# HGRN2 and differential attention on one core: Newton's steps on GpSimd, x's block sums behind the second head's gates, query weights split by VectorE, last heads' transposes with an earlier due time

## The chip, the cores and the metric

The kernel runs on one core of a Trainium2 chip. The time is the device time of one execution in microseconds (us), as the median of several runs. The core's engines work side by side, each through its own queue in order: TensorE (PE, matmuls and transposes), VectorE (DVE), ScalarE (ACT), GpSimd (POOL), and SyncE (SP), which starts most DMAs. They wait for each other by semaphores.

## What is computed

A trunk of two layers over 512 frames of 1024 features (float32, batch 1). The first layer mixes by a gated linear recurrence (HGRN2) of 8 heads, the second by differential attention of 8 heads over keys and values projected after layer one; a squared-ReLU MLP follows each. Every part has an RMS norm before and after. Cut to what matters here:

```python
def rms_norm(x, w):
    y = x * lax.rsqrt(jnp.mean(x * x, axis=-1, keepdims=True) + EPS)
    return y * w

def hgrn2_mixer(h, w_in, lb, gate_norm_w, w_out):
    q, f, i, g = jnp.split(h @ w_in, ...)
    q = silu(q); k = (1 - lb) * sigmoid(-f); log_f = ...
    o = hgrn2_recurrence(q, k, log_f, i)          # S_t = diag(f_t) S_(t-1) + k_t v_t^T, o_t = S_t^T q_t
    return (rms_norm(o, gate_norm_w) * silu(g)) @ w_out

def diff_attn_mixer(h, k, v, w_q, ...):
    o = softmax(q0 k0 + bias) v - lam * softmax(q1 k1 + bias) v
    return rms_norm(o, subln_w) * (1 - lam_init) @ w_out

for layer in range(2):
    h = h + rms_norm(mixer(rms_norm(h, pre)), post)
    h = h + rms_norm(mlp(rms_norm(h, mlp_pre)), mlp_post)
```

The norm of each head's output, in either mixer, and the norm of x at the very start need a reciprocal square root for each frame: a tile of 128 partitions by 4 numbers.

## The kernel before

Activations lie with features on the partitions and 512 frames along the free axis. A float32 product is made of three matmuls: weights and activations are each split into a high part (`whi`, `xhi`, `uhi`, rounded by a ScalarE copy) and a low part (`wlo`, `xlo`, `ulo`, the difference, a VectorE subtraction), and hi x hi, hi x lo and lo x hi are added up in PSUM.

The order of PE's instructions is written out by the class `Plan` (L45): a main generator, and chains that are spawned from it, each of which yields a number or a condition. The numbers are due times in estimated PE time: a chain whose time has come and whose condition holds goes on before the main generator does. The constants `W_...` (L30 to L36) are these due times. PE's order is kept as the plan issues it; the other engines' queues are ordered by a scheduler, with instructions of chains ahead of those of the main generator.

The stages that the change touches:

- **The start.** `first_loads` brings x and the first query weights; `start` (L735) squares x, sums the squares by matmuls (`ps_mc`), takes the reciprocal root `rcol` with `rsqrt_col` (L240), lays it on a diagonal `dg` (L755), and PE spreads it to `rb` with `ps_sp`. All gates of the heads need `rb`. Meanwhile PE works on the projections `qf` of heads 0 and 1 and the values `i`.
- **`rsqrt_col`** makes an estimate by integer arithmetic on the bits (L249) and three Newton steps of three VectorE operations each (L251 to L253). It is called once by `start` and 16 times by `head_norm` (L622), once for each head of either mixer. `head_norm` squares the head's output on ScalarE, calls it, scales the output (`os`, two quarters on VectorE, L632, two on ScalarE, L634), waits `W_HEAD` and transposes with PE (`hn`).
- **`block_sums`** (L695) makes sums and differences of blocks of x for the fast block products of the value and gate projections: eight ScalarE copies into `sums`, then a VectorE subtraction, three times four VectorE operations (`odd`), and four splits (`x0` to `x3`). It is spawned in the main generator (L1058) when `rb` is there.
- **HGRN heads.** `head` (L801) makes the gates, then goes through levels of block size 1 to 64: PE's scores `gl`, on VectorE the products of q and k with the decay (L849, L850) and a masked copy, on GpSimd the product of decays `tt` (L853). Two heads run interleaved. PE meanwhile goes on with projections: `i`, the gate `g` with weights `wg`, the next heads' `qf`.
- **Query weights.** Heads 0 to 3 split by `load_w` (ScalarE copy, VectorE subtraction); heads 4 to 7 by `load_d` (L204): a negated ScalarE copy into the low part, a copy into the high part, and a DMA from GpSimd's queue that adds the weight to the low part.

Of the kernel before, what the change touches and what calls it, by code (L numbers as in the profile page):

```python
# [14 lines left out]
ALU = mybir.AluOpType  # L15
# [16 lines left out]
W_NEW, W_NEWSUM, W_RSTD = 5.8, 9.7, 4.5  # L32
W_GATE_FIRST, W_GATE, W_LEVEL = 10.0, 5.7, 2.15
W_KEYS, W_STATE = 1.5, 0.8
W_HEAD, W_STORE = 11.7, 5.5
W_QK, W_NEXT, W_P, W_PER_TILE, W_PT = 3.6, 0.94, 5.0, 0.66, 2.5  # L36


# [50 lines left out]
def trunk_kernel(ctx: ExitStack, tc: tile.TileContext, x_t, w_qf, w_g, w_gs, w_i, w_is, w_ao, w_kv, w_q, w_bo, w_up, w_us, w_dn,  # L89
# [71 lines left out]
            nc.sync.dma_start(raw[:, i * n:(i + 1) * n, :], src[:, per * pr + i * n:per * pr + (i + 1) * n, :])  # L161
        return raw

    last_split = []

    def split_w(raw, gain, pr, name):

# [27 lines left out]
    def split_b(raw, name):  # L195
# [8 lines left out]
    def load_d(src, ncols, name):  # L204

        out = []
        per = 1024 // ncols
        for pr in range(ncols // 128):
            out += split_d(fetch_w(src, ncols, pr, name), src[:, per * pr:per * (pr + 1), :], f"{name}_{pr}")
        return out  # L210
# [29 lines left out]
    def rsqrt_col(ms, add, out, scale=1.0):  # L240

        n = ms.shape[1]
        x = cp.tile([P, 4], F32, tag="nx", name="nx", bufs=4)[:, :n]
        t = cp.tile([P, 4], F32, tag="nt", name="nt", bufs=4)[:, :n]
        if isinstance(add, float):
            v.tensor_scalar(x, ms, scale, add, op0=ALU.mult, op1=ALU.add)
        else:
            v.scalar_tensor_tensor(x, ms, scale, add, op0=ALU.mult, op1=ALU.add)
        v.tensor_scalar(out.bitcast(I32), x.bitcast(I32), -0.5, 1597463007.0, op0=ALU.mult, op1=ALU.add)  # L249
        for _ in range(3):  # L250
            v.scalar_tensor_tensor(t, out, -0.5, out, op0=ALU.mult, op1=ALU.mult)  # L251
            v.tensor_tensor(t, t, x, op=ALU.mult)
            v.scalar_tensor_tensor(out, t, 1.5, out, op0=ALU.add, op1=ALU.mult)  # L253

    def mean_cols(parts, n, ones):

# [362 lines left out]
                    else:  # L619
                        yield r  # L620

    def head_norm(pool, po, add, name):  # L622

        os = pool.tile([P, 4, P], F32, tag="os", name=f"os_{name}", bufs=2)
        ss = col("ss")
        for c in range(4):
            a.activation(os[:, c, :], po[:, c * P:(c + 1) * P], AF.Square, accum_out=ss[:, c:c + 1])
        y = col("yh")
        rsqrt_col(ss, add, y, 1.0 / P)
        for c in range(4):  # L630
            if c % 2 == 0:
                v.tensor_scalar(os[:, c, :], po[:, c * P:(c + 1) * P], y[:, c:c + 1], None, op0=ALU.mult)  # L632
            else:
                a.activation(os[:, c, :], po[:, c * P:(c + 1) * P], AF.Copy, scale=y[:, c:c + 1])  # L634
        yield W_HEAD
        pt = smt(f"hn_{name}")
        for c in range(4):
            pe.transpose(pt[:, c * P:(c + 1) * P], os[:, c, :], ident)
        yield pt
# [55 lines left out]
    def block_sums(xs, ts):  # L695

        gain = gn[:, G_APRE:G_APRE + 8]
        e, f = sums

        def split(src, sign, n):  # L700
            if n < 3:
                hi, lo = [wp.tile([P, 4, 256], F32R, tag=t, name=f"{t}_x{n}", bufs=8) for t in ("whi", "wlo")]
            else:
                hi, lo = [u[3].rearrange("p j (r t) -> p (j r) t", r=2) for u in (uhi, ulo)]
            a.activation(hi, src, AF.Copy, scale=sign)
            if sign > 0:
                v.tensor_tensor(lo, src, hi.bitcast(F32), op=ALU.subtract)
            else:
                v.scalar_tensor_tensor(lo, src, -1.0, hi.bitcast(F32), op0=ALU.mult, op1=ALU.subtract)
            ts.append([(hi[:, r, :], lo[:, r, :]) for r in range(4)])  # L710

        def odd(n, out, op):

            for r in range(4):
                v.scalar_tensor_tensor(out[:, r], xs[2 * r + 1][:, n * 256:n * 256 + 256], gain[:, 2 * r + 1:2 * r + 2],
                                       out[:, r], op0=ALU.mult, op1=op)

        for r in range(4):
            for n, t in enumerate((e, f)):
                a.activation(t[:, r], xs[2 * r][:, n * 256:n * 256 + 256], AF.Copy, scale=gain[:, 2 * r:2 * r + 1])  # L720
            yield 2.0
        v.tensor_tensor(e, e, f, op=ALU.subtract)
        split(e, 1.0, 0)
        yield 5.0
        odd(1, f, ALU.subtract)
        split(f, 1.0, 1)
        yield 5.0
        odd(1, e, ALU.add)
        split(e, -1.0, 2)
        yield 5.0  # L730
# [61 lines left out]
    def hgrn(hp, w0, xs):  # L792
# [8 lines left out]
        def head(h, pss):  # L801
            if h < 2:
# [8 lines left out]
                                   sg.rearrange("p (c t) -> p c t", c=4), op0=ALU.mult, op1=ALU.mult)  # L811
            v.tensor_tensor(qq.rearrange("p (c t) -> p c t", c=4), qc[:, :, 0:P],
                            tf.rearrange("p (c t) -> p c t", c=4), op=ALU.mult)
            a.activation(qc[:, :, P:192], qq.rearrange("p (c b two) -> p c b two", c=4, two=2)[:, :, :, 1], AF.Copy)
            yield W_GATE if h >= 2 else W_GATE_FIRST
            if h >= 2:
                yield until(("mix", h - 2))
# [70 lines left out]
                    pe.matmul(po[:, c * P:(c + 1) * P], qq[:, c * P:(c + 1) * P], st[:, c - 1, :], start=False, stop=True)  # L888
                yield 0
            done(("po", h))  # L890
            for pt in head_norm(hp, po, EPS, f"a{h}"):
                if isinstance(pt, float):
                    yield pt
            v.tensor_tensor(gg, pt, gg, op=ALU.mult)
# [130 lines left out]
        for p in range(4):  # L1025
            for h in (2 * p, 2 * p + 1):
                if h >= 3 and h % 2:
                    yield until(("rec", h - 3))
                wt = w0 if h == 0 else w1 if h == 1 else load_w(w_qf[h], 256, None, f"qf{h}") if h < 4 else load_d(w_qf[h], 256, f"qf{h}")
                pss = [mmt(f"qf{h}_{n}") for n in range(2)]  # L1030
                if h == 0:
                    w1 = load_w(w_qf[1], 256, None, "qf1")
                    done("w1")
                    for kt in range(8):
                        for n in (1, 0):
                            wmm(pss[n], wt, kt, n * P, xhi, xlo, 0, S, kt == 0, kt == 7)
                        yield 0
                else:
                    for n in (1, 0):
                        for kt in range(8):  # L1040
                            wmm(pss[n], wt, kt, n * P, xhi, xlo, 0, S, kt == 0, kt == 7)
                            yield 0
                spawn(head(h, pss))
            if p == 0:
# [10 lines left out]
                    for i in range(2):  # L1055
                        a.activation(vts[i][:, tt, :], ps[:, i * 256:(i + 1) * 256], AF.Copy, scale=rcol[:, tt:tt + 1])
                yield until("rb")
                spawn(block_sums(xs, ts), 2.0)  # L1058
                wt = load_w(w_g, 256, None, "wg")
                for j in range(2):  # L1060
                    ps = mmt(f"g0_{j}")
# [47 lines left out]
    def attention(ap, f):  # L1109
# [27 lines left out]
        def unit(h, qi, kq, vt, bt, po, mx):  # L1137
# [40 lines left out]
            if qi == 3:  # L1178

                ez = col("ez")  # L1180
                v.scalar_tensor_tensor(ez, mx[:, :, 2], EPS, mx[:, :, 2], op0=ALU.mult, op1=ALU.mult)
                for hn in head_norm(ap, po, ez, f"b{h}"):
                    if isinstance(hn, float):
                        yield hn
                store_u(h, hn)
                yield W_STORE
                done(("amix", h))
# [166 lines left out]
```

## Time and profile before

| | |
|---|---|
| median of 3 runs | 1273.94 us (1272.99 to 1274.47) |
| the profiled execution | 1273.18 us |
| its span in the trace | 1271.4 us |
| PE busy | 1240.0 us (98%) |
| VectorE busy | 825.8 us (65%) |
| ScalarE busy | 673.9 us (53%) |
| GpSimd busy | 95.6 us (8%), 166 instructions |
| mean granted clock of PE | 0.994 |

The span is the time between the first and the last instruction in the trace; the rest of the profiled execution's time lies around it. A granted clock of 1.00 is PE at full speed (2.4 GHz), 0.50 is the lower level (1.2 GHz). A row of the view in order of time gives the start, the duration, the engine, the line and the operation with what it writes and reads; in brackets stands how long the engine had been idle, and what ended that. The numbers of buffers and heads are left out of names there: `os_a` is the scaled output of an HGRN head, `os_b` of an attention head, `qf` the query and forget projections in HGRN, `kq` the key and query ones in attention.

### The profile page before, as it was taken

What the parts mean: (1) busy time and instruction counts of PE and PEld (TensorE: products, weight loads), DVE (VectorE), ACT (ScalarE), POOL (GpSimd) and SP (SyncE); (2) the same over time, 40 slices, a digit from 0 to 9 for tenths busy, and PEclk for the clock granted to TensorE, in tenths of its full rate; (3) what the DMA queues carried; (4) which work ended last, traced back from release to release, by engine and by line L of the source; (5) the groups of instructions that cost most, each with busy time, mean ns of one, the idle gap of its engine ahead of it and who ended that gap; (6) DMA issues with size and microseconds to landing.
All of it is one profiled execution on the core that took longest, in us unless ns stands there. A gap on an engine that the chain in (4) does not pass through costs nothing.

```text
span 1271.4 us, 21443 instructions
## 1 busy us (share of the span) xinstructions
PE 1240.0 (98%) x8440; PEld 1122.8 (88%) x8440; DVE 825.8 (65%) x1654; ACT 673.9 (53%) x1248; POOL 95.6 (8%) x166
## 2 busy tenths in 40 slices
PE   9999999999999999999999999999999999999996
PEld 7788898899988988989999787889998898988996
DVE  7768885866854654636488978664885463663645
ACT  7345546437751733715556877664773371561632
POOL 0102211210000000000100000001000000000000
PEclk9999999999999999999999999999999999999999
DMA  7223557342356663644616322313435355363521
GB/s 253 72 67 92 122 115 184 94 150 68 135 166 124 179 149 95 186 106 115 217 51 203 113 88 79 100 63 105 137 111 158 96 175 122 103 196 74 158 102 67
DMA packets 57303, 158.54 MB, mean 125 GB/s; under 512 B 6354, under 2 KB 8659, under 8 KB 57203
## 3 DMA queue, kind: packets, MB, share of 16 engines
q1 hardware_dynamic: 45920, 120.34, 30.2%
q0 software_dynamic: 11040, 36.71, 13.7%
q8 instruction: 66, 1.08, 0.4%
q14 instruction: 35, 0.28, 0.1%
q10 hardware_dynamic: 242, 0.13, 0.0%
HBM read 147.45 MB, written 9.70 MB: 124 GB/s over the span
## 4 chain that ended last, share of the span: by engine, by line
PE 79%; issue 6%; DMA 6%; DVE 5%; ACT 4%; POOL 0%; SPq 0%; DVEq 0%; ACTq 0%; POOLq 0%
PE dn L114 20%; PE qf L114 7%; PE up L114 7%; PE ux L114 6%; PE kq L114 6%; PE ao_h L114 3%; DMA raw_s<-in_w_us_dram 3%; PE bo_h L114 3%; PE dn_h L114 3%; PE uz L114 3%; PE gl L114 3%; PE v L114 3%; PE g L114 2%; PE lg L114 2%; PE i L114 2%
## 5 line engine op out<-in xcount | busy, mean ns | idle before, releaser
L114 PE MATMUL dn<-uhi,whi_dn 128*128 128x512 f32 x384 | 151.9, 396 | 0.0
L114 PE MATMUL dn<-ulo,whi_dn 128*128 128x512 f32 x384 | 151.9, 396 | 0.0
L114 PE MATMUL dn<-uhi,wlo_dn 128*128 128x512 f32 x384 | 151.9, 395 | 0.0
L200 ACT ACTIVATE whi_a<-raw_a 128x1024 fp32r<-128x1024 f32 x24 | 25.4, 1059 | 118.5 <-PE dn L114 115.6
L114 PEld LDWEIGHTS dn<-uhi,whi_dn 128*128 128x128 f32 x384 | 72.2, 188 | 17.8 <-ACT r L563 0.7
L114 PEld LDWEIGHTS dn<-uhi,wlo_dn 128*128 128x128 f32 x384 | 72.2, 188 | 17.3
L114 PEld LDWEIGHTS dn<-ulo,whi_dn 128*128 128x128 f32 x384 | 72.2, 188 | 16.9
L173 DVE TENSOR_TENSOR wlo_dn<-raw_dn,whi_dn 128x1024 fp32r<-128x1024 f32 x64 | 76.6, 1220 | 5.9 <-ACT whi_dn L172 4.6
L468 DVE TENSOR_TENSOR ulo<-r,uhi 128x1024 fp32r<-128x1024 f32 (+1 forms) x40 | 40.2, 1010 | 53.7 <-ACT uhi L467 53.7
L114 PE MATMUL up<-xhi,wlo_up 128*128 128x256 f32 x256 | 72.1, 281 | 1.0 <-DVE wlo_up L173 1.0
L114 PE MATMUL up<-xhi,whi_up 128*128 128x256 f32 x256 | 72.6, 284 | 0.0
L114 PE MATMUL up<-xlo,whi_up 128*128 128x256 f32 x256 | 71.8, 281 | 0.0
L172 ACT ACTIVATE whi_dn<-raw_dn 128x1024 fp32r<-128x1024 f32 x64 | 65.7, 1051 | 7.1 <-PE up L114 3.0
L114 PE MATMUL dn_h<-uhi,whi_dn 128*128 128x256 f32 x240 | 66.6, 278 | 0.0
L114 PE MATMUL dn_h<-ulo,whi_dn 128*128 128x256 f32 x240 | 66.3, 276 | 0.0
L114 PE MATMUL dn_h<-uhi,wlo_dn 128*128 128x256 f32 x240 | 66.3, 276 | 0.0
L610 DVE TENSOR_TENSOR zacc<-dn,zacc 128x512 f32<-128x512 f32 x32 | 22.1, 691 | 59.1 <-PE dn L114 59.0
L512 POOL DMA_DIRECT2D raw_s<-in_w_us_dram x24 | 20.8, 866 | 490.3 <-DMA raw_s<-in_w_us_dram 288.3
L114 PE MATMUL qf<-xhi,whi_qf 128*128 128x512 f32 x128 | 53.2, 415 | 1.7 <-ACT xhi L679 1.4
L114 PE MATMUL qf<-xhi,wlo_qf 128*128 128x512 f32 x128 | 51.4, 402 | 1.8 <-DMA wlo_qf<-in_w_qf_dram 1.7
L114 PE MATMUL qf<-xlo,whi_qf 128*128 128x512 f32 x128 | 51.4, 401 | 0.3 <-DVE xlo L680 0.3
L200 ACT ACTIVATE whi_t<-raw_a 128x1024 fp32r<-128x1024 f32 x24 | 25.5, 1061 | 49.4 <-PE dn L114 27.2
(531 smaller groups left out, 4133.8 us busy)
## 6 DMA issues: line engine op xcount, KB each, us to landing
raw_dn<-in_w_dn_dram SPq DMA_DIRECT2D x64, 512.0 KB, 4.5
raw_a<-in_w_us_dram SPq DMA_DIRECT2D x24, 512.0 KB, 4.3
raw_s<-in_w_us_dram SPq DMA_DIRECT2D x48, 256.0 KB, 4.4
raw_s<-in_w_us_dram POOLq DMA_DIRECT2D x24, 512.0 KB, 6.4
raw_up<-in_w_up_dram SPq DMA_DIRECT2D x16, 512.0 KB, 4.2
raw_wkv<-in_w_kv_dram SPq DMA_DIRECT2D x16, 512.0 KB, 3.7
raw_qf<-in_w_qf_dram SPq DMA_DIRECT2D x14, 512.0 KB, 4.8
raw_d<-in_w_us_dram SPq DMA_DIRECT2D x12, 512.0 KB, 4.3
```

Of the source, the lines that this page charges most:

```text
L114: nc.tensor.matmul(out, lhsT, rhs, **kw)
L172: last_split[:] = [a.activation(hi, raw, AF.Copy)]
L173: v.tensor_tensor(lo, raw, hi.bitcast(F32), op=ALU.subtract)
L200: a.activation(hi, raw, AF.Copy)
L468: v.tensor_tensor(ulo[pr][:, :, lo:hi], r, uhi[pr][:, :, lo:hi].bitcast(F32), op=ALU.subtract)
L512: g.dma_start(rs, ws[p, :, 0:2, :], accum_op=ALU.add)
L610: v.tensor_tensor(z, pss[n4], z, op=ALU.add)
```

## The change

Four things, in seven pieces of the source:

1. The Newton steps go to GpSimd, as four operations a step: square, product with x, `-0.5 t + 1.5`, product. The estimate stays on VectorE. For 17 calls, 153 VectorE operations leave and 204 on GpSimd come.
2. `block_sums` is spawned by head 1's gate, with the due time `W_GATE_FIRST` = 10, and its eight copies are held on ScalarE until head 1's last gate copy (`odd`, L814) is issued. Its later due times shrink from 5 to 3.
3. Heads 4 to 7 load their query weights with `load_w`: eight negated copies on ScalarE and eight adding DMAs on GpSimd's queue leave, and eight subtractions on VectorE come.
4. The transposes of the last head of each mixer get the due time 9.0 instead of 11.7.

```diff
-W_HEAD, W_STORE = 11.7, 5.5
+W_HEAD, W_HEAD_LAST, W_STORE = 11.7, 9.0, 5.5
...
         for _ in range(3):
-            v.scalar_tensor_tensor(t, out, -0.5, out, op0=ALU.mult, op1=ALU.mult)
-            v.tensor_tensor(t, t, x, op=ALU.mult)
-            v.scalar_tensor_tensor(out, t, 1.5, out, op0=ALU.add, op1=ALU.mult)
+            g.tensor_tensor(t, out, out, op=ALU.mult)
+            g.tensor_tensor(t, t, x, op=ALU.mult)
+            g.tensor_scalar(t, t, -0.5, 1.5, op0=ALU.mult, op1=ALU.add)
+            g.tensor_tensor(out, out, t, op=ALU.mult)
...
-    def head_norm(pool, po, add, name):
+    def head_norm(pool, po, add, name, last):
...
-        yield W_HEAD
+        yield W_HEAD_LAST if last else W_HEAD
...
+        def copies(r):
+            for n, t in enumerate((e, f)):
+                a.activation(t[:, r], xs[2 * r][:, n * 256:n * 256 + 256], AF.Copy, scale=gain[:, 2 * r:2 * r + 1])
...
         for r in range(4):
-            for n, t in enumerate((e, f)):
-                a.activation(t[:, r], xs[2 * r][:, n * 256:n * 256 + 256], AF.Copy, scale=gain[:, 2 * r:2 * r + 1])
+            with tc.issue_after(marks["a"].ins):
+                copies(r)
             yield 2.0
...
-        yield 5.0
+        yield 3.0
...
-            a.activation(qc[:, :, P:192], ..., AF.Copy)
+            odd = a.activation(qc[:, :, P:192], ..., AF.Copy)
+            if h == 1:
+                marks["a"] = odd
+                spawn(block_sums(xs, ts), W_GATE_FIRST)
...
-                wt = w0 if h == 0 else w1 if h == 1 else load_w(w_qf[h], 256, None, f"qf{h}") if h < 4 else load_d(w_qf[h], 256, f"qf{h}")
+                wt = w0 if h == 0 else w1 if h == 1 else load_w(w_qf[h], 256, None, f"qf{h}")
...
-                spawn(block_sums(xs, ts), 2.0)
```

What this does to the queues at three places. PE's own order is the same but for the four transposes `hn` of HGRN's head 7, which stand three matmuls earlier, and SP's is the same.

**VectorE at the start, from the estimate of `rcol` to the diagonal `dg`.** Before:

```order
L246 TENSOR_SCALAR nx<-ps_mc 128x4
L173 TENSOR_TENSOR wlo_wi_347<-raw_wi_344,whi_wi_346 128x1024
L249 TENSOR_SCALAR rcol<-nx 128x4
L173 TENSOR_TENSOR wlo_wg_596<-raw_wg_593,whi_wg_595 128x1024
L251 SCALAR_TENSOR_TENSOR nt<-rcol 128x4
L173 TENSOR_TENSOR wlo_wg_602<-raw_wg_599,whi_wg_601 128x1024
L252 TENSOR_TENSOR nt<-nt,nx 128x4
L707 TENSOR_TENSOR wlo_x_716<-sums_82,whi_x_715 128x1024
L253 SCALAR_TENSOR_TENSOR rcol<-nt,rcol 128x4
L173 TENSOR_TENSOR wlo_qf_0_727<-raw_qf_0_724,whi_qf_0_726 128x1024
L251 SCALAR_TENSOR_TENSOR nt<-rcol 128x4
L715 SCALAR_TENSOR_TENSOR sums_82<-xraw_74,gn,sums_82 128x256
```

After:

```order
L173 TENSOR_TENSOR wlo_wi_338<-raw_wi_335,whi_wi_337 128x1024
L238 TENSOR_SCALAR nx<-ps_mc 128x4
L173 TENSOR_TENSOR wlo_wi_344<-raw_wi_341,whi_wi_343 128x1024
L241 TENSOR_SCALAR rcol<-nx 128x4
L173 TENSOR_TENSOR wlo_wi_350<-raw_wi_347,whi_wi_349 128x1024
L748 TENSOR_SCALAR nrcol<-rcol 128x4
L752 TENSOR_TENSOR dg<-ident,rcol 128x512
L756 COPY rb<-ps_sp 128x512
```

The Newton operations (`nt`, `rcol`) stand on GpSimd, and the splits of the gate's weights (`wlo_wg`), of the sums (`wlo_x`) and of head 2's query (`wlo_qf`) between them are gone from here.

**VectorE behind level 16 of heads 0 and 1** (`q_385` and `k_379` before, `q_388` and `k_382` after, are head 1's; `gl_16` in the masked copy is the level). Before:

```order
L849 TENSOR_TENSOR q_385<-q_385,tt_469 128x16x16
L850 TENSOR_TENSOR k_379<-k_379,tt_469 128x16x16
L825 COPY_PREDICATED sc_462<-mask,gl_16_579 112x16x16
L707 TENSOR_TENSOR wlo_x_838<-sums_83,whi_x_837 128x1024
L849 TENSOR_TENSOR q_371<-q_371,tt_454 128x8x32
L850 TENSOR_TENSOR k_365<-k_365,tt_454 128x8x32
L825 COPY_PREDICATED sc_447<-mask,gl_32_609 96x8x32
L849 TENSOR_TENSOR q_385<-q_385,tt_469 128x8x32
L850 TENSOR_TENSOR k_379<-k_379,tt_469 128x8x32
```

After:

```order
L849 TENSOR_TENSOR q_388<-q_388,tt_472 128x16x16
L704 TENSOR_TENSOR wlo_x_597<-sums_83,whi_x_596 128x1024
L850 TENSOR_TENSOR k_382<-k_382,tt_472 128x16x16
L825 COPY_PREDICATED sc_465<-mask,gl_16_603 112x16x16
L712 SCALAR_TENSOR_TENSOR sums_82<-xraw_74,gn,sums_82 128x256
L712 SCALAR_TENSOR_TENSOR sums_82<-xraw_75,gn,sums_82 128x256
L712 SCALAR_TENSOR_TENSOR sums_82<-xraw_76,gn,sums_82 128x256
L712 SCALAR_TENSOR_TENSOR sums_82<-xraw_77,gn,sums_82 128x256
L173 TENSOR_TENSOR wlo_wg_620<-raw_wg_617,whi_wg_619 128x1024
L173 TENSOR_TENSOR wlo_wg_626<-raw_wg_623,whi_wg_625 128x1024
L849 TENSOR_TENSOR q_374<-q_374,tt_457 128x8x32
L850 TENSOR_TENSOR k_368<-k_368,tt_457 128x8x32
```

Four operations of the block sums and both splits of the gate's weights now stand between the levels of 16 and 32.

**VectorE around the norms of heads 0 and 1** (`os_a_777`, `os_a_809` before; `os_a_802`, `os_a_837` after). Before, from the end of the first chain:

```order
L246 TENSOR_SCALAR nx<-ss 128x4
L253 SCALAR_TENSOR_TENSOR yh<-nt,yh 128x4
L249 TENSOR_SCALAR yh<-nx 128x4
L632 TENSOR_SCALAR os_a_777<-o_769,yh 128x128
L251 SCALAR_TENSOR_TENSOR nt<-yh 128x4
L252 TENSOR_TENSOR nt<-nt,nx 128x4
L253 SCALAR_TENSOR_TENSOR yh<-nt,yh 128x4
L797 TENSOR_TENSOR k_882<-qf_1_737,rb 128x512
L251 SCALAR_TENSOR_TENSOR nt<-yh 128x4
L632 TENSOR_SCALAR os_a_777<-o_769,yh 128x128
L252 TENSOR_TENSOR nt<-nt,nx 128x4
L253 SCALAR_TENSOR_TENSOR yh<-nt,yh 128x4
```

After, the whole of it:

```order
L238 TENSOR_SCALAR nx<-ss 128x4
L241 TENSOR_SCALAR yh<-nx 128x4
L625 TENSOR_SCALAR os_a_802<-o_794,yh 128x128
L238 TENSOR_SCALAR nx<-ss 128x4
L241 TENSOR_SCALAR yh<-nx 128x4
L625 TENSOR_SCALAR os_a_802<-o_794,yh 128x128
L794 TENSOR_TENSOR k_897<-qf_1_762,rb 128x512
L625 TENSOR_SCALAR os_a_837<-o_829,yh 128x128
L803 TENSOR_SCALAR ek_898<-ek_898,oml,lb 128x512
L625 TENSOR_SCALAR os_a_837<-o_829,yh 128x128
L912 TENSOR_TENSOR raw_sgs_1019<-raw_sgs_1019 128x512
L913 TENSOR_TENSOR raw_sgs_1019<-raw_sgs_1019,raw_ags_1018 128x512
```

The second head's `nx` and estimate stand behind the first head's scaling, and head 2's `k` and `ek` behind and between the scalings.

**ScalarE at the same place.** Before:

```order
L634 ACTIVATE os_a_777<-o_769,yh 128x128
L798 ACTIVATE ek_883<-k_882 128x512
L634 ACTIVATE os_a_777<-o_769,yh 128x128
L805 ACTIVATE k_882<-k_882 128x512
L191 ACTIVATE whi_dgs_1018<-raw_sgs_1010 128x512
L634 ACTIVATE os_a_809<-o_801,yh 128x128
L190 ACTIVATE wlo_dgs_1019<-raw_sgs_1010 128x512
L634 ACTIVATE os_a_809<-o_801,yh 128x128
L200 ACTIVATE whi_sgs_1025<-raw_sgs_1010 128x1024
```

After:

```order
L627 ACTIVATE os_a_802<-o_794,yh 128x128 x2
L795 ACTIVATE ek_898<-k_897 128x512
L627 ACTIVATE os_a_837<-o_829,yh 128x128
L802 ACTIVATE k_897<-k_897 128x512
L627 ACTIVATE os_a_837<-o_829,yh 128x128
L191 ACTIVATE whi_dgs_1027<-raw_sgs_1019 128x512
L190 ACTIVATE wlo_dgs_1028<-raw_sgs_1019 128x512
L200 ACTIVATE whi_sgs_1034<-raw_sgs_1019 128x1024
```

The two copies of half weights (`whi_dgs`, `wlo_dgs`) stand behind both scalings of head 1. In attention the same happens once with the copy `at` of head 1's third query tile: it stood ahead of both ScalarE scalings of head 0, and stands behind the first of them.

## Rows read from the trace of the kernel before

**Rows 1.** the page: busy time (share of the span) and instructions of each engine

```profile
PE 1240.0 (98%) x8440; PEld 1122.8 (88%) x8440; DVE 825.8 (65%) x1654; ACT 673.9 (53%) x1248; POOL 95.6 (8%) x166
```

**Rows 2.** PE's waits: what PE waited for, total us, times, longest us

```profile
PE ps_sp L114 <- DVE dg L755: 3.0, 1, 3.0
PE qf L114 <- DMA wlo_qf<-in_w_qf_dram: 1.7, 1, 1.7
PE ao_h L114 <- ACT uhi L643: 1.4, 1, 1.4
PE qf L114 <- ACT xhi L679: 1.4, 1, 1.4
```

**Rows 3.** PE in order of time: start, us, operation [idle before <-releaser]

```profile
11.17 0.51 PE L114 MATMUL qf<-xhi,whi_qf 128*128 128x512 f32 x1 [1.38 <-ACT xhi L679]
...
40.11 2.07 PE L114 MATMUL ps_sp<-dg,ones 128*128 128x512 f32 x2 [3.04 <-DVE dg L755]
```

**Rows 4.** ScalarE in order of time, just before the first of these waits

```profile
9.60 0.91 ACT L720 ACTIVATE sums<-xraw,gn 128x256 f32<-128x256 f32 x2 [0.75 <-DMA xraw<-in_x_t_dram]
```

**Rows 5.** VectorE in order of time, from the first estimate to the diagonal

```profile
31.25 0.16 DVE L249 TENSOR_SCALAR rcol<-nx 128x4 int32<-128x4 int32 x1
31.32 1.22 DVE L173 TENSOR_TENSOR wlo_wg<-raw_wg,whi_wg 128x1024 fp32r<-128x1024 f32 x1
...
39.37 0.68 DVE L755 TENSOR_TENSOR dg<-ident,rcol 128x512 f32<-128x512 f32 x1
```

**Rows 6.** stretches: us, busy PE PEld DVE ACT POOL, granted clock, DMA share, GB/s

```profile
40.00:42.50 2.50, 2.39 (x4) 1.26 (x5) 0.33 (x2) 0.00 (x0) 0.00 (x0) 0.51 0.32 123
42.50:45.00 2.50, 2.50 (x11) 2.02 (x10) 2.47 (x5) 1.33 (x3) 0.00 (x0) 0.81 0.00 0
...
213.00:216.00 3.00, 3.00 (x26) 2.87 (x25) 1.21 (x4) 0.56 (x2) 0.00 (x0) 1.00 1.08 273
```

**Rows 7.** GpSimd in order of time, products of heads 2 and 3

```profile
102.53 0.65 POOL L853 TENSOR_TENSOR tt<-tt 128x4 f32<-128x4 f32 x1
...
115.37 0.20 POOL L853 TENSOR_TENSOR tt<-tt 128x8 f32<-128x8 f32 x1
...
115.65 0.20 POOL L853 TENSOR_TENSOR tt<-tt 128x4 f32<-128x4 f32 x1
```

**Rows 8.** VectorE in order of time, norms of heads 0 and 1

```profile
94.94 0.17 DVE L249 TENSOR_SCALAR yh<-nx 128x4 int32<-128x4 int32 x1
...
95.34 0.16 DVE L252 TENSOR_TENSOR nt<-nt,nx 128x4 f32<-128x4 f32 x1
95.54 0.16 DVE L253 SCALAR_TENSOR_TENSOR yh<-nt,yh 128x4 f32<-128x4 f32 x1
...
100.39 0.35 DVE L632 TENSOR_SCALAR os_a<-o,yh 128x128 f32<-128x128 f32 x1
...
101.70 0.69 DVE L912 TENSOR_TENSOR raw_sgs<-raw_sgs 128x512 f32<-128x512 f32 x1 [0.17 <-ACT wlo_dgs L190]
...
114.48 0.42 DVE L850 TENSOR_TENSOR k<-k,ek 128x256 f32<-128x256 f32 x1
```

**Rows 9.** PE in order of time, head 2's second level

```profile
116.35 0.99 PE L114 MATMUL gl<-q,k 128*126 128x64 f32 x8
```

**Rows 10.** VectorE in order of time, level 16 of head 1, and later

```profile
71.61 0.43 DVE L849 TENSOR_TENSOR q<-q,tt 128x256 f32<-128x256 f32 x1 [0.46 <-PE gl L114]
...
79.33 1.67 DVE L715 SCALAR_TENSOR_TENSOR sums<-xraw,gn,sums 128x256 f32<-128x256 f32 x4
```

**Rows 11.** PE in order of time, the gate's third matmul

```profile
72.56 0.39 PE L114 MATMUL g<-xhi,wlo_wg 128*128 128x512 f32 x1
```

**Rows 12.** ScalarE in order of time, attention's head 1, third tile

```profile
729.72 0.49 ACT L1171 ACTIVATE at<-pt 128x384 f32<-128x384 f32 x1
```

**Rows 13.** VectorE and PE in order of time, at the same place

```profile
727.38 0.17 DVE L249 TENSOR_SCALAR yh<-nx 128x4 int32<-128x4 int32 x1
...
729.82 0.31 PE L114 MATMUL lg<-kq,kq 128*128 128x128 f32 x1
```

More of the change, by code (lines that the diff above doesn't have):

```diff
@@ L162, in fetch_w @@
         return raw
-    last_split = []
+    last_split, marks = [], {}
     def split_w(raw, gain, pr, name):
@@ L202, in split_b @@
         return [(hi[:, i, :], lo[:, i, :]) for i in range(n)]
[L204 to L210, printed above, removed]
     def xpart(j, n):
@@ L723, in block_sums @@
         split(e, 1.0, 0)
-        yield 5.0
+        yield 3.0
         odd(1, f, ALU.subtract)
         split(f, 1.0, 1)
-        yield 5.0
+        yield 3.0
         odd(1, e, ALU.add)
         split(e, -1.0, 2)
-        yield 5.0
+        yield 3.0
         odd(0, e, ALU.subtract)
@@ L813, in head @@
                             tf.rearrange("p (c t) -> p c t", c=4), op=ALU.mult)
-            a.activation(qc[:, :, P:192], qq.rearrange("p (c b two) -> p c b two", c=4, two=2)[:, :, :, 1], AF.Copy)
+            odd = a.activation(qc[:, :, P:192], qq.rearrange("p (c b two) -> p c b two", c=4, two=2)[:, :, :, 1], AF.Copy)
+            if h == 1:
+                marks["a"] = odd
+                spawn(block_sums(xs, ts), W_GATE_FIRST)
             yield W_GATE if h >= 2 else W_GATE_FIRST
@@ L890, in head @@
             done(("po", h))
-            for pt in head_norm(hp, po, EPS, f"a{h}"):
+            for pt in head_norm(hp, po, EPS, f"a{h}", h == NH - 1):
                 if isinstance(pt, float):
@@ L1181, in unit @@
                 v.scalar_tensor_tensor(ez, mx[:, :, 2], EPS, mx[:, :, 2], op0=ALU.mult, op1=ALU.mult)
-                for hn in head_norm(ap, po, ez, f"b{h}"):
+                for hn in head_norm(ap, po, ez, f"b{h}", h == NH - 1):
                     if isinstance(hn, float):
```

## The prediction

> **What bounds the kernel now.** I read the page first. TensorE (PE) is busy 98% of the span, VectorE 65%, ScalarE 53%, GpSimd 8% [rows 1]. So a gain can only come from the few places where PE waits or is clocked low, and a loss comes from each new place where PE waits; the busy time that moves between the other engines has no price of its own. The list of PE's waits comes next [rows 2]: 3.0 us for the diagonal matrix `dg` at the start, 1.7 us for the accumulating DMA of a query weight, and twice 1.4 us for a split. In order of time the first of these are at 11.17 us and at 40.11 us [rows 3]. After the latter the granted clock reads 0.51 over 2.5 us and 0.81 over the next 2.5 us [rows 6]: 2.5 x 0.49 + 2.5 x 0.19 = 1.7 us lost, the lower of the two levels (1.2 GHz) being on for about 3.4 us. After the DMA wait of 1.7 us it stayed at 1.00 [rows 6]. So a new wait costs its length, and perhaps 1.7 us more. Then I read VectorE, ScalarE and GpSimd at the places where the changed order of instructions puts work behind a wait.
>
> **The price of a Newton step.** On VectorE two dependent small operations stand 0.20 us apart (95.34 and 95.54) [rows 8]: nine take 1.8 us alone. GpSimd has none of Newton's forms yet, but it has products of 128x8 and 128x4 numbers, each using the one before: 115.37 and 115.65, so 0.28 us apart [rows 7]. Beside a VectorE operation with two inputs the same 128x4 product took 0.65 us [rows 7]. The bounds for one of the twelve operations are 0.20 (VectorE's own) and 0.65 + 0.08 = 0.73 us. I take 0.28, the nearest row in size and engine: 12 x 0.28 = 3.4 us for a chain, 1.6 us more than before, plus some 0.1 us for each handing over. The Trainium skill ("GPSIMD Engine Reference", 3.1 Elementwise) gives GpSimd 1.96 times VectorE's time for a long two-input product; the rows here give 1.4 for small ones. By the page, 0.39 us an operation, the sum below would be some 8 us more.
>
> **Start: a gain.** Two things leave. The copies of `sums` at 9.60 us (0.91 us for the pair) stand on ScalarE just ahead of the split of x that PE waits for at 11.17 us [rows 3, 4]; they go behind head 1's gate, so that wait shrinks by about 0.85 us. And Newton for `rcol` is, on VectorE, strung between big operations of 1.22 us each: from the estimate at 31.25 to `dg` at 39.37 us, 8.1 us for a chain of 1.8 us [rows 5]. After the change the estimate comes at 31.25 - 0.85 = 30.4, GpSimd starts about 30.7 beside one last two-input split (its first operation may wait 1 us), needs 3.4 us and ends by 34 to 35; `dg` takes 0.68 us and is there by 36. PE arrives at 40.11 - 3.04 - 0.85 = 36.2 us. The wait of 3.04 us goes, and with it probably the low clock behind it: -3.04 - 0.85 - 1.7 = **-5.6 us**, bounds -3.9 (the low clock stays) and -7.3 (the one after 11 us goes as well).
>
> **Query weights: a gain.** PE's wait of 1.7 us for the accumulating DMA [rows 2] has no cause any more, **-1.7 us**. Eight splits of 1.22 us (the price of [rows 5]) come onto VectorE, and eight copies leave ScalarE. VectorE has idle time in these stages, except where a split is queued between two levels of a head (below). SP's queue is unchanged.
>
> **Last heads sooner: next to nothing.** PE's order is the same but for four transposes of HGRN's head 7, which move three matmuls ahead: **-0.35 us** of the wait for `uhi` [rows 2]; the transposes of attention's head 7 don't move. A Newton chain longer by 1.6 us still ends before them.
>
> **The gate's weights: a loss.** The block sums used to be worked at the start; now their VectorE operations come in the middle of the heads' levels, and the split of `wlo_wg`, done at 31.32 us before [rows 5], is queued behind them. In the new order there stand, behind head 1's level of 16: q, `wlo_x` , k, a masked copy, four `sums`, and only then `wlo_wg`. The first of these can't start before PE's scores, 71.61 us [rows 10]. With 0.43 us for a small one, 1.22 for a split and 1.67 for the four sums [rows 5, 10]: 71.61 + 3 x 0.43 + 1.22 + 1.67 + 1.22 = 77.0, less some 0.4 for overlap, 76.6 us. PE wants it at 72.56 us [rows 11]: **+4.1 us**. (Both ends move with the start's gain.) Bounds 3.6 to 4.6.
>
> **Heads 0 and 1: a loss.** VectorE works in order, so the scaling `os` that needs Newton's result now blocks it while GpSimd works, and the second head's estimate stands behind the first head's scaling: two chains in a row. From the first estimate's end, 95.1 us [rows 8]: 95.1 + 0.1 + 3.4 = 98.6 for the first scaling; 0.7 us for it and the second head's estimate; 0.1 + 3.4 again: 102.85 for the second head's scaling, which was at 100.39 [rows 8], +2.5. Behind it ScalarE now has both its scalings ahead of the two half-weight copies (0.6 us each) for which VectorE's 101.70 operation waits: +1.3, so 3.7 us in all. The product of k at 114.48 us (0.42 long) is then ready at 118.6; PE uses it at 116.35 [rows 8, 9]: +2.3 to 2.7, I take 2.5. At the next level VectorE has the new query split and two operations of head 3 (1.14 + 0.67 + 0.6 us) ahead of what PE waits for, part of which is covered: +1.7. Together **+4.2 us**, bounds 2 and 8.
>
> **Heads 4 and 5** repeat the pattern (it stands twice in the trace, with the same distances), the second part mostly covered: **+2.9 us**, bounds 1 and 6. **Heads 2, 3, 6, 7** have single chains, with 2.5 to 4.3 us between the scaling and its transposes; the splits in VectorE's queue are not hidden everywhere: **+1.3**, bounds 0 and 5.
>
> **Attention.** For head 0 the result on GpSimd comes at 727.38 + 0.17 + 0.1 + 3.4 = 731.05 us [rows 13]. ScalarE's copy of the transposed scores at 729.72 [rows 12] now stands behind a scaling that waits for it: it starts some 2.2 us late, its PSUM buffer is what PE's scores at 729.82 [rows 13] need next: +2.0. The same once more between heads 6 and 7: +1.5. Heads 1 to 5 had 4.6 to 6.4 us from estimate to scaling already and have 2 to 5 us of room. **+3.5 us**, bounds 0 and 8.
>
> **Sum.** -5.6 - 1.7 - 0.35 + 4.1 + 4.2 + 2.9 + 1.3 + 3.5 = +8.35 us. Of the three new waits longer than 2 us one, I think, also drops the clock, as after 40.11 us: +1.7, so +10. The profiled execution had 1273.18 us, 0.76 under the median of 1273.94; 1273.94 + 10 = **1284 us**.
>
> **Rivals.**
> 1. *GpSimd's small operations are as quick as VectorE's.* The products in rows 7 are the nearest, but not the same. Six chains lie on the path with nothing over them (heads 0 and 1, 4 and 5, and two in attention); each is 12 x 0.08 = 1 us shorter at 0.20 us an operation, -5.8, and the clock doesn't drop: 8.35 - 5.8 = +2.5, less another 2 if the start's low clock after 11 us goes too: 1274.5, not slower. It decides from about 0.21 us an operation. If in addition the wait for `wlo_wg` is covered, 1270, which is faster. Against it: the rows' 0.28. Chance 0.17, a third of it faster.
> 2. *The two engines block each other.* A 128x4 product of 0.20 us took 0.65 beside a two-input VectorE operation [rows 7]. The Trainium skill ("SBUF — State Buffer", section on the two separate sides) says that the port pair they share is an exclusive lock, taken "for the whole instruction"; the trace agrees, 0.65 for 0.20. In heads 0, 1, 4 and 5 VectorE stands still during a chain, so it can't block it; in the other eleven it works on. At 0.73 us a chain takes 8.8 us there, 3 to 4 more than those heads had; that exceeds their room of 2 to 5 us in about half of them, by 2 us each, and two more drops of the clock: 10 + 5 x 2 + 3.4 = +23, 1297 us. Chance 0.22.
> 3. *The heads' chains are hidden* (the stall of 101.70 is absorbed by ScalarE's waits): then 8.35 - 4.2 - 2.9 = +1.3 and 1275, no change that can be told. I count it in the 0.17 above.
>
> **How the numbers follow.** The forecast has 0.61, as 1277 to 1292; the second rival 0.22, 1292 to 1305; the first and third 0.17, 1268 to 1277. A measurement of this kernel tells about 0.2%, 2.5 us, from no change. Slower by more 0.83, within 0.11, faster 0.06. The range that leaves out a tenth on either side is 1274 to 1300 us.
>
> **What would show it.** PE's waits should no longer list `dg` or the DMA of `wlo_qf`; they should list `wlo_wg` with about 4 us, the scores `gl` with k from VectorE, some 2.5 us twice, and in attention `lg` with a ScalarE copy. GpSimd's small operations should stand 0.28 us apart. I am wrong if `wlo_wg` is early, if the operations stand 0.2 us apart, or if they often take over 0.5 us.

## The result, and the profile after

| | before | after |
|---|---|---|
| median | 1274.09 us (1272.99 to 1274.47, 4 runs) | 1284.61 us (1283.17 to 1286.03, 4 runs) |
| the profiled execution | 1273.18 us | 1284.99 us |
| its span | 1271.4 us | 1283.2 us |

After over before is 1.0084, 95% interval 1.0067 to 1.0101: 0.84% slower, 10.5 us. The forecast was 1284 us.

The page of after, busy times (against [rows 1]):

```profile
PE 1241.9 (97%) x8440; PEld 1123.2 (88%) x8440; DVE 814.8 (63%) x1509; ACT 666.2 (52%) x1240; POOL 138.0 (11%) x362
```

GpSimd's busy time rose by 42.4 us (204 Newton operations, less eight DMA issues), VectorE's fell by 11.0 us and ScalarE's by 7.7 us. PE's fell in share only because the span grew: it works 1.9 us longer, part of it at the lower clock, and stands still for the rest. As in the kernel before, only PE's waits tell anything. What PE waited for after, total us, times, longest (against [rows 2]):

```profile
PE gl L114 <- DVE k L850: 5.2, 4, 2.0
...
PE g L114 <- DVE wlo_wg L173: 3.6, 1, 3.6
PE lg L114 <- DVE mx L1154: 2.5, 3, 0.9
PE lg L114 <- ACT at L1170: 2.0, 1, 2.0
PE kt L119 <- DVE k L850: 2.0, 2, 1.7
...
PE ao_h L114 <- ACT uhi L636: 1.1, 1, 1.1
```

The waits for `dg` and for the DMA of `wlo_qf` are gone from the list. New are `gl` and `kt` (scores and key transposes of HGRN heads, waiting for VectorE's product of k), `g` (the gate, waiting for its weights' low part), and `lg` (attention's scores). A wait `ux` in the MLPs, 3.9 us in all before and 4.1 after, stands in both lists; the change doesn't touch it. To place the new ones I took the start of the same PE instruction in both traces, median over six neighbours, and looked at where the difference after minus before steps:

| place | after minus before, us | step | forecast |
|---|---|---|---|
| start, to the last values | 0 to -7.50 | -7.5 | -5.6 |
| gate weights at 69.1 us, and the low clock behind | -7.50 to -1.15 | +6.35 | +4.1 |
| heads 0 and 1 (scores of head 2) | -1.14 to 2.63 | +3.8 | +4.2 |
| heads 2, 3, 6, 7 | five steps of 0.2 to 1.9 | +4.5 | +1.3 |
| query weights of head 6 | 5.01 to 3.01 | -2.0 | -1.7 |
| heads 4 and 5 (scores of head 6) | 3.00 to 5.14 | +2.1 | +2.9 |
| HGRN's last transposes, and what follows | 7.26 to 5.32 | -1.95 | -0.35 |
| first MLP, keys and values | 5.30 to 6.19 | +0.9 | 0 |
| attention | 6.18 to 12.0 | +5.8 | +3.5 |
| second MLP | 12.0 to 11.78 | -0.2 | 0 |

The steps add up to 11.8 us, the difference of the two spans. The sum of the forecast's terms was 8.35, and 1.7 on top for one stretch of low clock. The table is of one execution of each kernel: in the MLPs, where nothing was changed, single steps of up to 1.8 us come and go, and so do short stretches of low clock, some 1.6 us each (the mean granted clock of the kernel before lay between 0.991 and 0.998 over its executions).

**The start.** GpSimd, VectorE and PE in order of time (against [rows 3, 5]):

```profile
28.86 1.10 POOL L243 TENSOR_TENSOR nt<-rcol 128x4 f32<-128x4 f32 x1 [28.40 <-DVE rcol L241]
30.04 0.19 POOL L244 TENSOR_TENSOR nt<-nt,nx 128x4 f32<-128x4 f32 x1
...
32.83 0.20 POOL L246 TENSOR_TENSOR rcol<-rcol,nt 128x4 f32<-128x4 f32 x1
...
33.14 0.69 DVE L752 TENSOR_TENSOR dg<-ident,rcol 128x512 f32<-128x512 f32 x1
...
34.28 1.02 PE L114 MATMUL ps_sp<-dg,ones 128*128 128x512 f32 x2
```

A chain of twelve took 4.17 us here: one operation of 1.10 us beside the two-input split of VectorE, eleven at 0.28 us apart. `dg` is there at 33.8, PE comes at 34.28 and doesn't wait.

**The gate weights.** VectorE, PE, and two stretches with the granted clock (0.50 and 0.69) behind the wait (against [rows 10, 11]):

```profile
66.25 1.67 DVE L712 SCALAR_TENSOR_TENSOR sums<-xraw,gn,sums 128x256 f32<-128x256 f32 x4
67.83 2.36 DVE L173 TENSOR_TENSOR wlo_wg<-raw_wg,whi_wg 128x1024 fp32r<-128x1024 f32 x2
...
69.10 0.80 PE L114 MATMUL g<-xhi,wlo_wg 128*128 128x512 f32 x1 [3.57 <-DVE wlo_wg L173]
...
69.00:72.00 3.00, 2.90 (x12) 2.56 (x13) 2.02 (x5) 1.90 (x3) 0.00 (x0) 0.50 0.51 152
72.00:75.00 3.00, 3.00 (x16) 2.54 (x14) 2.56 (x6) 1.06 (x1) 0.00 (x0) 0.69 0.57 201
```

The four `sums`, then `wlo_wg`, and PE stands for 3.57 us. The clock was at its lower level (1.2 GHz) for 6.83 us from 67.02 on (the other such stretches before the span's last microseconds lasted 3.41 us each); 4.75 us of them lie behind 69.10, where PE works.

**Heads 0 and 1.** VectorE, then PE, then a stretch with the granted clock (0.57) behind the wait (against [rows 8, 9]):

```profile
97.36 0.35 DVE L625 TENSOR_SCALAR os_a<-o,yh 128x128 f32<-128x128 f32 x1 [3.39 <-POOL yh L246]
...
101.37 0.35 DVE L625 TENSOR_SCALAR os_a<-o,yh 128x128 f32<-128x128 f32 x1 [2.22 <-POOL yh L246]
...
104.04 0.69 DVE L912 TENSOR_TENSOR raw_sgs<-raw_sgs 128x512 f32<-128x512 f32 x1 [1.47 <-ACT wlo_dgs L190]
...
116.77 0.50 DVE L850 TENSOR_TENSOR k<-k,ek 128x256 f32<-128x256 f32 x1
...
117.32 1.15 PE L114 MATMUL gl<-q,k 128*126 128x64 f32 x8 [1.96 <-DVE k L850]
...
122.33 0.98 PE L114 MATMUL gl<-q,k 128*124 128x64 f32 x8
...
118.00:122.00 4.00, 4.00 (x23) 4.00 (x23) 4.00 (x8) 1.02 (x2) 0.00 (x0) 0.57 0.59 178
```

VectorE waits 3.39 us for the first chain (`[3.39 <-POOL yh]`) and 2.22 us for the second, then 1.47 us for ScalarE's half weights; its product of k comes at 116.77, 2.3 us later than before though PE is 1.1 us ahead there, and PE's scores wait 1.96 us. Behind the wait the clock was at its lower level for 3.41 us from 118.22 on. At the next level (122.33) PE doesn't wait. So the step of 3.8 us is 2.2 us at the wait and 1.6 us of low clock.

### The profile page after: what moved, and what is told of

Read it like the earlier page. It is cut to its first block, busy times and chain, and to the rows that moved or that the text cites. A ratio compares the mean times of both kernels' runs of the same rounds, so it can differ in the third digit from the quotient of the medians.

```text
span 1283.2 us, 21445 instructions
## 1 busy us (share of the span) xinstructions
PE 1241.9 (97%) x8440; PEld 1123.2 (88%) x8440; DVE 814.8 (63%) x1509; ACT 666.2 (52%) x1240; POOL 138.0 (11%) x362
## 5 line engine op out<-in xcount | busy, mean ns | idle before, releaser
L114 PEld LDWEIGHTS gl<-q,k 128*112 128x112 f32 (+5 forms) x384 | 42.3, 178 | 9.6 <-DVE k L850 5.8
```

The source lines that it names most:

```text
L114: nc.tensor.matmul(out, lhsT, rhs, **kw)
```

## The experiments

Each run is compared with the kernel before on the same chip, whose median was 1273.57 us for the first four and 1271.08 us for the others. So ratios are to be compared, not times.

### Newton back on VectorE

```diff
-            g.tensor_tensor(t, out, out, op=ALU.mult)
-            g.tensor_tensor(t, t, x, op=ALU.mult)
-            g.tensor_scalar(t, t, -0.5, 1.5, op0=ALU.mult, op1=ALU.add)
-            g.tensor_tensor(out, out, t, op=ALU.mult)
+            v.scalar_tensor_tensor(t, out, -0.5, out, op0=ALU.mult, op1=ALU.mult)
+            v.tensor_tensor(t, t, x, op=ALU.mult)
+            v.scalar_tensor_tensor(out, t, 1.5, out, op0=ALU.add, op1=ALU.mult)
```

> The changed kernel with only the Newton steps put back on VectorE. My theory: the chains on GpSimd cost about 12 us in the heads (PE's offset against the kernel before grows by 3.5 at heads 0 and 1, 2.1 at 4 and 5, 1.9 at 2 and 3, 3.4 at attention's head 0 and some 2.3 at later ones), and the start keeps its gain without them, because the big VectorE operations between the Newton steps have left with the block sums: 1270 us, 1267 to 1273. Rival: the heads lose because eight query splits crowd VectorE, and GpSimd's steps are what frees the start: 1280 us or more, with dg on the list of waits again.

Measured: 1269.67 us, ratio 0.9968 (0.9955 to 0.998), 0.32% faster than before, where the changed kernel is 0.84% slower. What PE waited longest for, and VectorE at the start:

```profile
PE g L114 <- DVE wlo_wg L173: 3.6, 1, 3.6
...
28.84 1.22 DVE L173 TENSOR_TENSOR wlo_wi<-raw_wi,whi_wi 128x1024 fp32r<-128x1024 f32 x1
29.97 0.15 DVE L243 SCALAR_TENSOR_TENSOR nt<-rcol 128x4 f32<-128x4 f32 x1
...
31.82 0.68 DVE L751 TENSOR_TENSOR dg<-ident,rcol 128x512 f32<-128x512 f32 x1
```

Of the changed kernel's new waits only that for `wlo_wg` is left at its size: `kt` is gone, the longest `gl` is 0.50 us and the longest `lg` 0.77 us. None is for `dg`: the last split is at 28.84, the Newton operations follow it 0.2 us apart, and `dg` is there at 32.5, earlier than with GpSimd (33.8). So GpSimd's Newton is a loss of about 1.2% (the two ratios) in the heads and brings nothing more at the start once the big operations have left from between the steps. The wait for `wlo_wg` is unchanged at 3.6 us.

### Newton on GpSimd alone

The kernel before with the same lines changed the other way.

> The kernel before with only the Newton steps on GpSimd. My theory: the losses in the heads stay (12 us), the wait for dg goes here too (two splits of 1.2 us instead of the whole chain stand ahead of it), with its low clock, 4.7 us: 1274 + 12 - 4.7 = 1281 us, 1278 to 1285. Rival (the losses need the other parts): 1270 us.

Measured: 1283.78 us, ratio 1.0082 (1.0059 to 1.0105). Two of PE's waits that the kernel before doesn't have:

```profile
PE gl L114 <- DVE k L851: 5.4, 4, 1.9
...
PE lg L114 <- ACT at L1172: 2.0, 1, 2.0
```

These waits are also the changed kernel's (5.2 and 2.0 us), here without its other parts. In PE's offsets the start gains 3.9 us (PE waits 0.30 us for `dg` in place of 3.04), and all that follows loses 15.6 (from -3.9 to 11.65), more than the 12 us of the theory; two stretches of low clock of 3.41 us each, from 115.60 and 170.22 on, are in it. So against the wait for `dg` either move is enough: GpSimd's steps alone, or the block sums' leaving alone (below). The rival, that the other parts are needed for the loss, falls.

### The block sums moved alone

```diff
+            odd = a.activation(qc[:, :, P:192], ..., AF.Copy)
+            if h == 1:
+                marks["a"] = odd
+                spawn(block_sums(xs, ts), W_GATE_FIRST)
...
-                spawn(block_sums(xs, ts), 2.0)
```

and the held copies and the shorter due times of `block_sums`, as in the change.

> The kernel before with only the block sums moved. My theory: the start gains 7.3 us although Newton is on VectorE, and the wait for wlo_wg at PE's first gate matmuls takes 6.3 back (3.6 of waiting, the rest low clock): 1273 us, 1271 to 1275. Rival (the start's gain is GpSimd's): dg still makes PE wait 2 to 3 us, 1277 to 1280 us.

Measured: 1272.61 us, ratio 0.9993 (0.9977 to 1.0009): no difference. PE's longest wait:

```profile
PE g L114 <- DVE wlo_wg L173: 3.6, 1, 3.6
```

PE's offset goes to -6.9 us at the start and back to 0 behind this wait. The move of the block sums wins and gives back the same amount; the rival falls, no wait for `dg` is left.

### The query splits alone

```diff
-                wt = w0 if h == 0 else w1 if h == 1 else load_w(w_qf[h], 256, None, f"qf{h}") if h < 4 else load_d(w_qf[h], 256, f"qf{h}")
+                wt = w0 if h == 0 else w1 if h == 1 else load_w(w_qf[h], 256, None, f"qf{h}")
```

> The kernel before with only the query weights of heads 4 to 7 split by VectorE. My theory: the wait for the accumulating DMA goes, -1.7 to -2.0: 1272 us, and no new wait above 0.5 us. Rival (eight subtractions of 1.2 us stand between two levels and PE waits for k): 1274 to 1277 us.

Measured: 1271.51 us, ratio 0.9985 (0.9969 to 1.0001): the time is as forecast, but at the edge of what a measurement tells. The mechanism is so only in part. In the trace the step at head 6 is -2.0 us, but +0.7 and +0.9 us come at heads 2 and 3, where PE waits for VectorE: 0.50 us at 119.19 for a product of k and 0.66 us at 155.09 for a state, against the theory's "no new wait above 0.5 us". The two waits stand, with the same lengths, in the four other traces with these splits and the heads' Newton steps on VectorE, and in no trace without the splits: so they are the splits' price, and the rival was right about the waits, if not about the time. The splits' own net is 0.4 us of gain, which lies inside the interval too; most of the rest of this trace's gain is low clock that didn't come. The wait for `dg` stands as before, and yet the granted clock behind it stayed at 1.00, where it was 0.51 in the kernel before [rows 6]:

```profile
PE ps_sp L114 <- DVE dg L755: 3.0, 1, 3.0
...
PE o L114 <- DVE st L881: 0.7, 1, 0.7
...
PE gl L114 <- DVE k L850: 0.5, 1, 0.5
...
40.00:42.50 2.50, 1.97 (x7) 1.32 (x8) 1.25 (x3) 0.00 (x0) 0.00 (x0) 1.00 0.41 150
```

### The gate weights split early

The run with Newton on VectorE, and the load of the gate's weights written out behind the first tile of values:

```diff
                     if tt == 0:
                         yield until("rcol")
+                        wt = load_w(w_g, 256, None, "wg")
...
                 yield until("rb")
-                wt = load_w(w_g, 256, None, "wg")
```

> As the run with Newton back on VectorE, and the load and split of the gate's weights written out right behind the first tile of values instead of behind all four, so that both splits stand between the Newton steps of rcol. My theory: PE's wait for wlo_wg (3.6 us) and the low clock behind it (2 to 2.8 us) go; dg comes 2.3 us later than in that run, where it had 1.9 us to spare, so 0 to 0.5 us of waiting for dg: 1269.7 - 6 = 1264 us, 1262 to 1266. Rival: dg's wait and its low clock come back (2 us and 1.7 us), 1268 us; or the wait for wlo_wg was hiding another one behind it, 1267 to 1270.

Measured: 1262.33 us, ratio 0.9923 (0.99 to 0.9947), with the next run the best of all: 0.77% faster than before. PE's longest wait in total, VectorE and PE at the start, and the first gate matmul with `wlo_wg`:

```profile
PE ao L114 <- ACT at L1169: 1.2, 3, 0.6
...
30.14 1.22 DVE L173 TENSOR_TENSOR wlo_wg<-raw_wg,whi_wg 128x1024 fp32r<-128x1024 f32 x1
...
32.56 1.23 DVE L173 TENSOR_TENSOR wlo_wg<-raw_wg,whi_wg 128x1024 fp32r<-128x1024 f32 x1 [0.34 <-issue]
...
34.37 0.68 DVE L751 TENSOR_TENSOR dg<-ident,rcol 128x512 f32<-128x512 f32 x1
...
35.11 1.12 PE L114 MATMUL ps_sp<-dg,ones 128*128 128x512 f32 x2 [0.42 <-DVE dg L751]
...
65.98 0.39 PE L114 MATMUL g<-xhi,wlo_wg 128*128 128x512 f32 x1
```

The splits stand between the Newton steps (30.14 and 32.56), `dg` is late by 0.42 us, and at 65.98 PE doesn't wait. The only low clock in this trace lies in the last 9 us of the span. Against the first run the ratio is lower by 0.45 points, 5.7 us: this is what the late split cost, and the reason that the block sums alone brought nothing. (In PE's offsets against that run the wait and its low clock give 5.7 us, and `dg` takes 0.8 us back; this execution, 1259.02 us, is also faster in the MLPs, where nothing was changed.)

### Newton of the start alone on GpSimd

The run before it, with `rsqrt_col` on GpSimd for `rcol` only.

> As the run before it, with the three Newton steps of rcol alone on GpSimd (the 16 of the heads stay on VectorE). My theory: 3.3 us of chain plus some 1 to 2 us beside the two-input splits, one split of 1.2 us instead of two ahead of dg: the same within 0.7 us as that run. Rival (GpSimd is what makes the start short): 2 us or more faster than that run.

Measured: 1261.77 us, ratio 0.9927 (0.9904 to 0.995), the same as the run before it. VectorE, and PE:

```profile
33.74 0.69 DVE L757 TENSOR_TENSOR dg<-ident,rcol 128x512 f32<-128x512 f32 x1
...
34.48 1.13 PE L114 MATMUL ps_sp<-dg,ones 128*128 128x512 f32 x2 [0.30 <-DVE dg L757]
```

`dg` comes 0.63 us earlier, but in this execution PE is 0.5 us earlier too (from 10 us on, before any Newton step), and still waits 0.30 us for it, against 0.42. Once the block sums have left, it doesn't matter at the start which engine does the steps.

### Two steps instead of three

The changed kernel with `range(2)`: the last Newton step is left out.

> The changed kernel with two Newton steps on GpSimd instead of three (8 operations a chain instead of 12, 2.2 us instead of 3.3; the last step of the reciprocal root is left out). My theory: VectorE and ScalarE stand behind a chain, so PE's loss shrinks by the shorter chain where chains are on the path: some 2 us each at heads 0 and 1 and at 4 and 5 (two chains in a row), 1.1 each at attention's head 0 and at about three other heads: 1284.6 - 8 = 1277 us, 1274 to 1279. Rival (the loss is the fixed cost of handing over and of the new order, whatever the length): 1282 us or more.

Measured: 1275.04 us, ratio 1.0032 (1.0016 to 1.0048), against 1.0084 with three: 0.52 points, 6.6 us, for four operations less in each chain. PE's waits:

```profile
PE gl L114 <- DVE k L850: 3.0, 2, 1.9
...
PE lg L114 <- ACT at L1170: 1.5, 1, 1.5
...
120.68 1.05 PE L114 MATMUL gl<-q,k 128*124 128x64 f32 x8 [1.06 <-DVE k L850]
```

The loss goes with the length of the chain. Where no low clock interferes, PE's offset against the changed kernel steps by -2.1 at heads 4 and 5 (two chains in a row), by -1.1 at head 6's chain and by -1.1 at attention's heads 4 and 6 (0.28 x 4 = 1.12 us a chain). At three places the low clock mixes in, so that they say less about the chain: at heads 0 and 1 the first wait is gone (-2.2) and so is the low clock of 118.22 (-1.6), but now PE waits 1.06 us at the second level (+1.3); behind heads 2 and 3 this execution has a wait of 1.90 us in place of 1.19 and a low clock of its own from 171.19 on (+2.3 in all); at attention's head 0 the wait is 1.54 in place of 2.05 us (-0.5) and the low clock behind it is absent (-1.5). The rival (a fixed cost of the new order) falls by its time, 1282 us or more. What the waits that are left owe to the remaining eight operations, to the handing over and to the query splits was not separated.

### The later due time

The run with Newton on VectorE, with 11.7 in place of 9.0 for the last heads, in one execution.

> As the run with Newton back on VectorE, with the last heads' due time back at 11.7. My theory: only HGRN's head 7 differs: its four transposes stand three matmuls later, and PE's wait for uhi is 1.4 instead of 1.1 us; nothing else moves, 1270 us. Rival: the earlier transposes are what removes the low clock behind that wait, and PE falls back 1.7 us more there.

Measured: 1268.35 us in its one run. PE's wait for `uhi`:

```profile
PE ao_h L114 <- ACT uhi L635: 1.4, 1, 1.4
```

1.4 against 1.1 us in the run that it differs from, and no low clock behind it in either. The fourth part of the change is worth 0.3 us, as the order of instructions said, and too little to be measured in the time.

## Why the prediction was right, point by point

**The Newton price: right.** The chosen 0.28 us an operation was read from products of decays; in the changed kernel the operations stand 0.28 us apart, and eleven of the seventeen chains took 3.27 to 3.29 us (forecast 3.4). The first rival (0.20 us) falls. The Trainium skill's 1.96 ("GPSIMD Engine Reference", 3.1 Elementwise) was measured for an addition of 2048 numbers a partition; for these small operations the traces have 1.4 (0.28 and 0.20 us apart).

**The start: direction and mechanism right, mis-sized, and the credit misplaced.** -7.5 instead of -5.6: the low clock after 11 us went too, the bound that I had named. The forecast let GpSimd free the start; that is one of two ways. The first run shows that the chain on VectorE is just as short once the block sums have left, and the run with Newton alone that GpSimd's chain does it without their leaving (0.30 us of the wait are left). That the low clock behind `dg` goes with the wait was not sure either: with the query splits alone the wait stood and the low clock was absent.

**The gate weights: the mechanism right, the size short by a clock.** The wait was 3.57 us (4.1 forecast). I had counted one low clock of 1.7 us over all new waits; this one alone had 6.83 us of low clock, and the step is 6.35 us.

**Heads 0 and 1, 4 and 5: right at the first level, and the sum partly by luck.** +3.8 and +2.1 for 4.2 and 2.9. At head 2's first level all is as forecast: 2.2 us for 2.5. The second part, 1.7 us of waiting at the next level behind the query split, was not there: k was ready at 121.94 us, and PE, slowed by the low clock, came for it at 122.33. The 1.6 us of that low clock stand in its place. In the run with two steps, which had neither the first wait nor this low clock, PE waits 1.06 us at that level; so the crowding is real, and the clock hid it here. At heads 4 and 5 the step is the first level's wait alone. The third rival, that these chains are hidden, falls with them.

**The other HGRN heads: mis-sized**, +4.5 for 1.3. I had judged them by the room between a scaling and its own transposes, and that room holds. What I had not looked at is what else stands behind the scaling on VectorE. GpSimd, VectorE and PE in after, head 6's norm and head 7's keys:

```profile
272.70 1.77 POOL L243 TENSOR_TENSOR nt<-yh 128x4 f32<-128x4 f32 x1 [27.31 <-DVE yh L241]
...
272.53 0.68 DVE L941 TENSOR_TENSOR g<-g,egs3-1_2533 128x512 f32<-128x512 f32 x1
273.13 1.28 DVE L176 SCALAR_TENSOR_TENSOR wlo_ao<-raw_ao,gn,whi_ao 128x1024 fp32r<-128x1024 f32 x1
277.58 0.35 DVE L625 TENSOR_SCALAR os_a<-o,yh 128x128 f32<-128x128 f32 x1 [3.17 <-POOL yh L246]
...
278.65 0.55 PE L119 MATMUL kt<-ident,k 128*128 128x128 f32 x3 [1.71 <-DVE k L850]
```

The chain's first operation took 1.77 us, beside two VectorE operations with two inputs one after the other; VectorE then waited 3.17 us for the result before head 6's scaling, with head 7's last products of q and k queued behind it, and PE's key transposes of head 7 waited 1.71 us. It is the same at heads 2 and 3: VectorE waits 2.57 and 2.32 us for their chains with products of k queued behind, and PE falls back 0.5 and 1.4 us.

**Attention: mechanism right, short by 2.3 us.** At head 0 all is as forecast, ScalarE's `at` behind the scaling and PE 2.05 us late (the first three rows). Behind it came a low clock of 3.41 us, which makes that step 3.4; with Newton alone on GpSimd the same wait of 2.05 us came without it. The two others, 1.1 us each, came at heads 4 and 6 and not at 6 alone; the other rows are of head 4:

```profile
737.56 0.37 ACT L627 ACTIVATE os_b<-ao,yh 128x128 f32<-128x128 f32 x1 [1.64 <-DVE os_b L625]
737.83 0.48 ACT L1170 ACTIVATE at<-pt 128x384 f32<-128x384 f32 x1
...
738.36 0.58 PE L114 MATMUL lg<-kq,kq 128*128 128x128 f32 x3 [2.05 <-ACT at L1170]
...
820.07 1.19 POOL L244 TENSOR_TENSOR nt<-nt,nx 128x4 f32<-128x4 f32 x1
...
819.91 1.29 DVE L176 SCALAR_TENSOR_TENSOR wlo_bo<-raw_bo,subg,whi_bo 128x1024 fp32r<-128x1024 f32 x1 [0.20 <-ACT whi_bo L175]
...
824.09 0.35 DVE L625 TENSOR_SCALAR os_b<-ao,yh 128x128 f32<-128x128 f32 x1 [1.89 <-POOL yh L246]
...
825.23 0.94 PE L114 MATMUL lg<-kq,kq 128*128 128x512 f32 x3 [0.84 <-DVE mx L1154]
```

The second Newton operation took 1.19 us; it ended 0.06 us behind the split of 1.29 us on VectorE that began just before it. VectorE stood 1.89 us before the scaling, and the scores' maxima (`mx`) came behind it. At head 6 the chain was undisturbed (3.29 us), VectorE stood 2.06 us, and PE lost as much: so it is the standing that costs, more than the longer chain. The Trainium skill ("SBUF — State Buffer", the section on the two separate sides) says that one engine holds the shared pair of ports for its whole instruction; 1.10, 1.77 and 1.19 us for operations that take 0.20 elsewhere agree.

**The second rival: half right.** The engines do block each other: six of the seventeen chains had operations of 0.5 to 1.8 us. But a chain lost 0.35 to 1.6 us by it, not the 5.4 that I priced: it met only one or two big operations of VectorE with both inputs in SBUF (the memory of the tiles), because VectorE soon came to the scaling itself and stood still. And not every two-input operation blocks: beside products that read one input from PSUM, where PE had left it (`k<-qf,rb` at 148.08 us, `kf<-kq,rb` at 753.38), the chain's operations took their 0.20 us. So the term "at 0.73 us a chain takes 8.8" was wrong, as an upper end that no chain came near. (The heads other than 0, 1, 4 and 5 have twelve chains, not eleven.)

**Query weights and last heads: right**, -2.0 for -1.7, and 0.3 for 0.35. Of the splits' price elsewhere, 1.6 us when they are alone, the forecast had the part at the second level (above) and not that at 155 us. A further 1.6 us at HGRN's end is a low clock that the kernel before had at 289 us and the changed one had not. It isn't the due time that removes it: it is absent in the runs with the early and with the late due time and in that with the query splits alone, and there in that with the block sums alone. What decides it stays open.

So the total was hit partly by luck: the start and the end of HGRN gave 3.5 us more than forecast and the paired heads cost 1.2 us less, while the gate weights, the other heads and attention cost 7.7 us more, for which only the 1.7 us of one low clock had been added. Much of it is the clock: the kernel before had three short stretches at the lower level, none of which is left, and three others came.

## What to carry to other kernels

A chain of small operations moved to an idle engine is no cheaper for being off the busy one: an engine that works in order and needs the result stands still while the other works, and everything queued behind it is late, other heads' work included. Look for what stands behind the consumer, not only for the consumer's own deadline. When work is moved from one stage to another, look also for what was done in passing before, here the gate's splits, and is now queued behind it; putting that one load back early was worth 0.45%.

## What the runs showed of the hardware

Small operations on 128 x 4 numbers that depend on each other stood 0.28 us apart on GpSimd (0.20 us each) and 0.20 us apart on VectorE (0.16 each). Where such a GpSimd operation began beside a big VectorE operation with both inputs in SBUF, it ended 0.06 us behind it, or behind a second one that followed at once (0.49 to 1.77 us in place of 0.20, in six chains of the changed kernel); beside VectorE products with one input in PSUM it took its 0.20 us. The granted clock was at its lower level for 6.83 us at PE's wait of 3.57 us, in all five traces with that wait; after waits of 1.4 to 3.04 us it fell for 3.41 us in some traces and not in others, after the wait of 3.04 us for `dg` in the kernel before and not in the run with the query splits alone.
